# Half of layer 0's first feed-forward group as seven products, narrower score and value products, and an explicit order for the operand forms

## The chip, the cores and the metric

The kernel runs on one core of a Trainium2 chip. The engines of a core run side by side, each through its own instruction list: TensorE (PE, with its weight loads shown as PEld), VectorE (DVE), ScalarE (ACT), GpSimd (POOL) and SyncE (SP). SP and POOL also hold the queues from which transfers between HBM and on-chip memory (SBUF) are issued. TensorE adds its products up in PSUM, where the kernel keeps eight tiles of 512 floats per partition (banks). The metric is the device time of one execution in microseconds, the median of several runs.

## The reference

A trunk of two layers works on 512 tokens of width 1024. Each layer has eight stick-breaking attention heads and four differential attention heads, an output projection, and a feed-forward block of width 4096 with a squared ReLU. All data is float32.

```python
for l in range(DEPTH):
    h = rmsnorm(x, attn_norm[l])
    proj = jnp.einsum('bsd,de->bse', h, w_in[l])
    sb_q, sb_k, sb_v, df_q, df_k, df_v = jnp.split(proj, splits, axis=-1)
    sb_out = stick_breaking_attention(...)        # w = exp(log_beta + sums of log_keep), out = w v
    df_out = ...                                  # softmax(q1 k1) - lam * softmax(q2 k2), times v, rmsnorm
    x = x + jnp.einsum('bse,ed->bsd', mixed, w_o[l])
    h = rmsnorm(x, mlp_norm[l])
    u = jnp.square(jax.nn.relu(jnp.einsum('bsd,df->bsf', h, w_ff1[l])))
    x = x + jnp.einsum('bsf,fd->bsd', u, w_ff2[l])
return rmsnorm(x, final_norm)
```

## The kernel before

**Numbers.** Every operand of a product is held as two float32r tiles, `hi` (a rounded copy, made by ACT) and `lo` (what is left of the number, made by DVE). `three` (lines 294 to 299) issues hi·hi, hi·lo and lo·hi into one PSUM bank, so each product is three matmuls. A weight tile of 128x1024 floats comes by DMA and is split by `_Weights.split_part` (lines 117 to 132): ACT writes `whi` at line 115, DVE writes `wlo` at line 131. At most four split weights stand ahead of their use. ACT and DVE therefore do one split for every weight that PE uses.

**Layout.** x is kept transposed, as eight chunks of 128 features by 512 tokens. The attention part interleaves dense projections with attention steps by a written-out clock (`attn`, `dense`). A score product (`scores`, lines 522 to 529) for query block i is 128(i+1) keys wide, but at least 256. The transposed weights of keys 256 to 511 lie in `zh` and `zl`, whose first 128 columns are zeros (lines 346 to 348), so that the last value product (`s3`, line 634) is 256 wide as well.

**Feed-forward.** A layer's feed-forward is done in four groups of 1024 features. The second matrix of every group, and the first matrix of groups 1 to 3, are multiplied by a scheme that needs seven products of half-size blocks instead of eight. Each of the seven ("forms", named 11, x3, x2, 21, x1, x4, 22) has a weight that is one block or a sum or difference of blocks, and an activation that is one block or a combination too. `quad_group` (lines 1018 to 1065) does this for half a group's first matrix: seven forms in the order of `FORMS`, each of 8 x 3 matmuls that are 256 wide, into three banks X, V and Y. Between them ACT copies Y from X (line 1038), which has to be done before form x2 adds to X, and DVE and ACT form the squared ReLU and its combinations.

Group 0 does its first matrix plainly: eight blocks (`block`, lines 307 to 312) of 8 x 3 matmuls that are 512 wide. After each block `evict_whole` (lines 946 to 963) takes the ReLU, the square and the forms of the result, and `h_form` (lines 983 to 1006) makes a part of the activation forms that groups 1 to 3 need. In layer 0 these differences are written over x itself, which was saved to a DRAM tile `park` before (lines 939 to 941).

**Weights of the seven products.** `bring` (lines 876 to 890) fetches the five buffers a to e of one half group. Role "e" (the buffer `norms`, which held the sum of squares) is filled by a load from SP's queue and then by a second transfer that adds another block to it, issued from POOL's queue (line 888); role "b" (`first_b`) likewise. Form x3 uses e. Then DVE adds e to a (`add`, line 893), which gives x2's weight. The forms of the second matrix have adding transfers on the same POOL queue (`fetch`, line 856, for its x3; `grow`, line 863).

**Order.** A scheduler puts the instructions on the engines in an order that follows its own estimate of readiness; each engine then runs its list strictly in that order. `behind(a, b)` forces a to stand after b on its engine.

Of the kernel before, what the change touches and what calls it, by code (L numbers as in the profile page):

```python
# [36 lines left out]
MAN = ()  # L37
_CTX = {}
# [50 lines left out]
_FIRST = [(l, g, j, q) for l in range(L) for g in range(1, GROUPS) for j in range(2) for q in QUADS]  # L89


class _Weights:
    def __init__(self, nc, dram, rawp, splp):
        self.nc, self.dram, self.rawp = nc, dram, rawp
        self.loaded = self.split = self.used = self.turn = 0
        self.raw, self.tiles, self.home, self.then = {}, {}, {}, {}
        self.depth = 3
        self.limit = len(_RING) // L
        self.eager = False
        self.pools = [splp]  # L100
        self.owner = {}
        self.rest_of = {}
# [35 lines left out]
    def do_split(self, n, ahead=None):  # L138
        while self.split < min(n, len(_UNITS)):
            i = self.split  # L140
            kind = _UNITS[i][0]
            if ahead is not None and i > ahead and self.owner.get(self.spot(i), -1) >= ahead:
                break
            if kind not in "fs":
                self.load(_SLOT[i] + 1)
            self.split_part(i, 0, 1024)
            self.rest_of[i] = self.last[1]
# [16 lines left out]
def trunk(ctx, tc, opened, xT, w, w2, w1, gfin, lamv, cos, sin, out):  # L164
# [71 lines left out]
    def split(hi, lo, src):  # L236
        a = nc.scalar.activation(hi, src, AF.Copy)  # L237
        nc.vector.tensor_tensor(out=lo, in0=src, in1=hi.bitcast(F32), op=ALU.subtract)  # L238
        return a

    def split_less(hi, lo, src):
        a = nc.scalar.activation(hi, src, AF.Copy, scale=-1.0)
        nc.vector.scalar_tensor_tensor(
            out=lo, in0=src, scalar=-1.0, in1=hi.bitcast(F32), op0=ALU.mult, op1=ALU.subtract)
        return a
# [48 lines left out]
    def three(pt, a, b, first, last, goes_on=False):  # L294
        ah, al = a
        bh, bl = b
        nc.tensor.matmul(pt, ah, bh, start=first, stop=False, skip_group_check=goes_on)  # L297
        nc.tensor.matmul(pt, ah, bl, start=False, stop=False, skip_group_check=goes_on)  # L298
        nc.tensor.matmul(pt, al, bh, start=False, stop=last, skip_group_check=goes_on)  # L299
# [7 lines left out]
    def block(name, tag="mm"):  # L307
        pt = bank(tag, name)
        u = W.next("px" if name[0] == "p" else "1")
        for c in range(KC):  # L310
            three(pt, wpair(u, c), hpair(c), c == 0, c == KC - 1)
            yield pt if c == KC - 1 else None
# [20 lines left out]
    for l in range(L):  # L333
        with ExitStack() as actx:
# [11 lines left out]
            zh, zl = (ap_.tile([P, 512], F32R, tag=f"z{n}", name=f"z{n}{l}") for n in "hl")  # L346
            nc.gpsimd.memset(zh[:, 0:128].bitcast(F32), 0.0)
            nc.gpsimd.memset(zl[:, 0:128].bitcast(F32), 0.0)
# [256 lines left out]
            def s2(u, also):  # L605
# [11 lines left out]
                if half:  # L617
                    split(xh[:, 384:896], xl[:, 384:896], pts[0])
                    split(zh[:, 128:512], zl[:, 128:512], pts[1][:, 128:512])
# [122 lines left out]
            def wo(half):  # L742
                for j in range(4):
                    u = W.next("o")
                    for dd in range(2):
# [10 lines left out]
                        if half == 0:  # L756
                            make_h(db, gcol("mlp", l, db))
                            add_sq(db, db == 0, tt, nc.vector)
# [77 lines left out]
        with ExitStack() as fctx:  # L836
# [35 lines left out]
            groups = [(g, j) for g in range(1, GROUPS) for j in range(2)]  # L872
# [25 lines left out]
            def let_load():  # L898
                W.limit += len(_RING) // L if not last else 0
# [45 lines left out]

            def evict_whole(pt, k):
                pair, which = k // 2, k % 2
                F = spots["de"[pair % 2]].rearrange("p (a t) -> p a t", a=4)
                hi, lo = (e[:, :, pair % 2, :] for e in sides[pair // 2])
                t = F[:, 2 * which : 2 * which + 2, :].rearrange("p a t -> p (a t)")  # L950
                nc.scalar.activation(t, pt, AF.Relu)
                nc.scalar.activation(t, t, AF.Square)
                if which == 0:
                    split(hi[:, 0, :], lo[:, 0, :], F[:, 1, :])
                    return
                split(hi[:, 1:3, :], lo[:, 1:3, :], F[:, 2:4, :])
                tt2(F[:, 1, :], F[:, 1, :], F[:, 0, :], ALU.subtract)
# [19 lines left out]
            def scaled(out, c0, half, other, op):  # L977
                for c in range(4):
                    nc.vector.scalar_tensor_tensor(
                        out=out[:, c, :], in0=x[:, c0 + c, half], scalar=gcol("mlp", l, c0 + c), in1=other[:, c, :],  # L980
                        op0=ALU.mult, op1=op)

            def h_form(k):
                if k == 1:
                    for c in range(4):
                        nc.scalar.activation(ta[:, c, :], x[:, c, early], AF.Copy, scale=gcol("mlp", l, c))
                    if last:
                        scaled(tb_, 0, late_, ta, ALU.subtract)
                elif k == 2:
                    scaled(tc_, 4, early, ta, ALU.subtract)  # L990
                    if not last:
                        scaled(tb_, 0, late_, ta, ALU.subtract)
# [10 lines left out]
                for form, at in (("x3", 6 if last else 3), ("21", 7 if last else 5)):  # L1003
# [14 lines left out]
            def quad_group(g, j, banks_):  # L1018
# [8 lines left out]
                for form in FORMS:  # L1027
# [3 lines left out]
                    for pr in range(2):  # L1031
                        for c in range(4):
                            at = 512 * pr + P * c
                            three(to[:, 256 * pr : 256 * pr + 256], (u[0][:, at : at + P], u[1][:, at : at + P]),
                                  (h[0][:, c, :], h[1][:, c, :]),
                                  form in ("11", "x3") and pr == c == 0, pr == 1 and c == 3, True)
                    if form == "11":
# [26 lines left out]
                    if j and form in ("11", "x3", "x2"):  # L1064
# [113 lines left out]
            for g in range(GROUPS):  # L1178
# [7 lines left out]
                else:  # L1186
                    for k in range(2 * GP):
                        for n, pt in enumerate(block(f"f{l}_{g}_{k}", "any")):
                            if (k, n) == (1, 0):
                                rms_square(ssq, f"m{l}")  # L1190
                        evict_whole(pt, k)
                        h_form(k)
# [3 lines left out]
                    p_, q_, r_, s_ = ring[0] % 3, 3, (ring[0] + 1) % 3, (ring[0] + 2) % 3  # L1196
                    held_on = {"Y": [bank("t", f"Y{l}{r}") for r in range(2)], "V": [bank("mm", f"V{l}{r}") for r in range(2)]}
                chains = {"X": [temp(k, f"X{l}{g}{k}") for k in (p_, q_)], **held_on}
                for form in FORMS2:
# [47 lines left out]
                    if g and form in ("11", "x3"):  # L1247
# [113 lines left out]
```

## Time and profile before

| | |
|---|---|
| median of 3 runs | 1128.51 us (1127.95 to 1129.98) |
| profiled execution, whole time | 1129.41 us |
| profiled execution, span from first to last instruction | 1127.6 us |
| TensorE busy | 1118.6 us, 99% |
| VectorE busy | 904.9 us, 80% |
| ScalarE busy | 686.8 us, 61% |
| GpSimd busy | 148.1 us, 13% |
| DMA moved | 181.28 MB, 161 GB/s on average |

The busy time of an engine is the time in which at least one of its instructions runs. Matmuls overlap in the pipeline, so what one costs in a row of them is the distance from its start to the next one's, not its duration. "Idle before ... <-" in a row names what ended the engine's idle time before it.

### The profile page before, as it was taken

To read this page: it belongs to the slowest core of one execution; us is meant where nothing else is said; L and a number is where in the kernel's file an instruction comes from. 1 tells how busy PE (TensorE), PEld (TensorE's weight loads), DVE (VectorE), ACT (ScalarE), POOL (GpSimd) and SP (SyncE) were. 2 spreads that over 40 slices of the span, in tenths; PEclk is the share of its full clock that TensorE was granted. 3 is DMA by queue.
4 is the path that set the end of the run, shared out by engine and by line. 5 is a ranking of instruction groups with operands and counts; after the bars stand their busy time and mean duration, and the time that the engine had idled before them with its cause. 6 is when DMAs were issued, how large, how long until landed. Compare 5 with 4: busy or idle time off the path is not lost.

```text
span 1127.6 us, 17680 instructions
## 1 busy us (share of the span) xinstructions
PE 1118.6 (99%) x6613; PEld 990.2 (88%) x6613; DVE 904.9 (80%) x1317; ACT 686.8 (61%) x1115; POOL 148.1 (13%) x233
## 2 busy tenths in 40 slices
PE   9999999999999999999999999999999999999997
PEld 7899889878899899899888998898888998998986
DVE  7897788788658878779878977887876787797787
ACT  6456666567558458466344666665765484674665
POOL 1001343101011001001000013330010110010010
PEclk9999999999999999999999999999999999999999
DMA  7665363259777678757326643622477886687462
GB/s 253 157 181 150 88 175 103 76 192 242 191 205 178 174 209 179 190 139 206 112 75 187 169 132 112 166 78 75 149 183 218 209 187 178 184 187 202 116 131 94
DMA packets 61045, 181.28 MB, mean 161 GB/s; under 512 B 7456, under 2 KB 8736, under 8 KB 60960
## 3 DMA queue, kind: packets, MB, share of 16 engines
q1 hardware_dynamic: 50160, 141.84, 40.3%
q0 software_dynamic: 10368, 37.75, 19.2%
q8 instruction: 52, 0.85, 0.3%
q10 hardware_dynamic: 432, 0.56, 0.1%
q14 instruction: 33, 0.27, 0.1%
HBM read 150.77 MB, written 4.19 MB: 137 GB/s over the span
## 4 chain that ended last, share of the span: by engine, by line
PE 97%; DVE 1%; issue 1%; DMA 0%; ACT 0%; POOL 0%; SPq 0%; POOLq 0%; DVEq 0%
PE X L297 9%; PE X L298 9%; PE X L299 9%; PE V L297 4%; PE V L298 4%; PE V L299 4%; PE wo L297 3%; PE wo L299 3%; PE wo L298 3%; PE f L298 2%; PE f L299 2%; PE f L297 2%; PE Y L297 2%; PE Y L299 2%; PE Y L298 2%; PE W L299 1%
## 5 line engine op out<-in xcount | busy, mean ns | idle before, releaser
L115 ACT ACTIVATE whi<-q 128x1024 fp32r<-128x1024 f32 x96 | 101.6, 1059 | 109.8 <-PE X L299 37.9
L131 DVE TENSOR_TENSOR wlo<-q,whi 128x1024 fp32r<-128x1024 f32 x96 | 117.0, 1222 | 49.4 <-ACT whi L115 49.4
L115 ACT ACTIVATE whi<-raw 128x1024 fp32r<-128x1024 f32 (+1 forms) x82 | 80.9, 992 | 46.6 <-issue 20.3
L131 DVE TENSOR_TENSOR wlo<-raw,whi 128x1024 fp32r<-128x1024 f32 (+1 forms) x82 | 95.4, 1169 | 10.4 <-ACT whi L115 10.0
L297 PE MATMUL X<-whi,Ah 128*128 128x512 f32 x248 | 97.6, 394 | 0.0
L298 PE MATMUL X<-wlo,Ah 128*128 128x512 f32 x248 | 96.6, 390 | 0.0
L299 PE MATMUL X<-whi,Al 128*128 128x512 f32 x248 | 96.6, 389 | 0.0
L131 DVE TENSOR_TENSOR wlo<-waves,whi 128x1024 fp32r<-128x1024 f32 x40 | 48.9, 1222 | 17.0 <-ACT whi L115 16.8
L115 ACT ACTIVATE whi<-waves 128x1024 fp32r<-128x1024 f32 x40 | 42.2, 1055 | 31.0 <-PE X L299 18.2
L297 PEld LDWEIGHTS X<-whi,Ah 128*128 128x128 f32 x248 | 46.6, 188 | 11.9 <-DVE y L1091 1.9
L299 PEld LDWEIGHTS X<-whi,Al 128*128 128x128 f32 x248 | 46.6, 188 | 9.8
L298 PEld LDWEIGHTS X<-wlo,Ah 128*128 128x128 f32 x248 | 46.6, 188 | 8.8
L299 PE MATMUL X<-h_hi,wlo 128*128 128x256 f32 x192 | 54.3, 283 | 0.0
L297 PE MATMUL X<-hxh,whi 128*128 128x256 f32 x192 | 54.3, 283 | 0.0
L298 PE MATMUL X<-hxl,whi 128*128 128x256 f32 x192 | 54.3, 283 | 0.0
L299 PE MATMUL X<-hxh,wlo 128*128 128x256 f32 x192 | 54.3, 283 | 0.0
L298 PE MATMUL X<-h_lo,whi 128*128 128x256 f32 x192 | 54.3, 283 | 0.0
L297 PE MATMUL X<-h_hi,whi 128*128 128x256 f32 x192 | 54.3, 283 | 0.0
L298 PE MATMUL f<-h_lo,whi 128*128 128x512 f32 x128 | 49.9, 390 | 0.5 <-DVE h_lo L249 0.5
L297 PE MATMUL f<-h_hi,whi 128*128 128x512 f32 x128 | 50.4, 394 | 0.0
L299 PE MATMUL f<-h_hi,wlo 128*128 128x512 f32 x128 | 49.9, 390 | 0.0
L238 DVE TENSOR_TENSOR Al<-x,Ah 128x512 fp32r<-128x512 f32 (+1 forms) x60 | 46.6, 793 | 3.8 <-ACT Ah L237 3.5
(748 smaller groups left out, 3794.9 us busy)
## 6 DMA issues: line engine op xcount, KB each, us to landing
raw<-in_w SPq DMA_DIRECT2D x78, 512.0 KB, 3.8
q<-in_w SPq DMA_DIRECT2D x48, 512.0 KB, 4.8
q<-in_w POOLq DMA_DIRECT2D x48, 512.0 KB, 7.8
waves<-in_w SPq DMA_DIRECT2D x28, 512.0 KB, 4.9
first_a<-in_w SPq DMA_DIRECT2D x12, 512.0 KB, 4.4
first_b<-in_w SPq DMA_DIRECT2D x12, 512.0 KB, 5.2
first_c<-in_w SPq DMA_DIRECT2D x12, 512.0 KB, 4.3
first_b<-in_w POOLq DMA_DIRECT2D x12, 512.0 KB, 7.1
```

What stands on the lines that cost most here:

```text
L115: return self.nc.scalar.activation(o, src, AF.Copy)
L131: self.last = h, nc.vector.tensor_tensor(out=lo[:, a:b], in0=raw[:, a:b], in1=hi[:, a:b].bitcast(F32), op=ALU.subtract)
L238: nc.vector.tensor_tensor(out=lo, in0=src, in1=hi.bitcast(F32), op=ALU.subtract)
L297: nc.tensor.matmul(pt, ah, bh, start=first, stop=False, skip_group_check=goes_on)
L298: nc.tensor.matmul(pt, ah, bl, start=False, stop=False, skip_group_check=goes_on)
L299: nc.tensor.matmul(pt, al, bh, start=False, stop=last, skip_group_check=goes_on)
```

## The change

Half of group 0's first matrix in layer 0 becomes a `quad_group` too: `WHOLE = (4, 8)` says that layer 0 does four plain blocks instead of eight, and then one half group by seven products. Layer 1 keeps its eight blocks. The weights for the four blocks that go are no longer in the plain list; five buffers are brought by `bring(0, ...)` in their place, and because these would have carried the squared ReLU of the plain blocks, the `y` tiles take that instead (`spread`). In layer 0 the activation forms, spread over blocks 1 to 7 before, are made after blocks 0 to 3, and the forms of the squared ReLU later than before (`forms_of`, called with x3's block and inside `quad_group`). Score products of the first query block and the last value product become 128 wide, and the zero columns go; an unused tile `zpad` keeps their room. A number of `behind` calls fix the order of the new forms on ACT and DVE.

```diff
+WHOLE = (GP, 2 * GP)
...
+def _by_seven(l, g):
+    return range(0 if g else WHOLE[l] // GP, 2)
...
             if g == 0:
-                units.extend(("1", l, f) for f in range(2 * GP))
-            else:
-                units.extend(("s", l, g, j, form) for j in range(2) for form in FORMS)
+                units.extend(("1", l, f) for f in range(WHOLE[l]))
+            units.extend(("s", l, g, j, form) for j in _by_seven(l, g) for form in FORMS)
...
-            zh, zl = (ap_.tile([P, 512], F32R, tag=f"z{n}", name=f"z{n}{l}") for n in "hl")
-            nc.gpsimd.memset(zh[:, 0:128].bitcast(F32), 0.0)
-            nc.gpsimd.memset(zl[:, 0:128].bitcast(F32), 0.0)
+            zh, zl = (ap_.tile([P, 384], F32R, tag=f"z{n}", name=f"z{n}{l}") for n in "hl")
+            ap_.tile([P, 256], F32, tag="zpad", name=f"zpad{l}")
...
-                wd = P * (i + 1)
-                wp = max(wd, 256)
+                wp = P * (i + 1)
...
-                        (1, 2): ((zh, zl), 256, 256, 256), (1, 3): ((zh, zl), 0, 256, 256)}[(half, kb)]
+                        (1, 2): ((zh, zl), 128, 256, 256), (1, 3): ((zh, zl), 0, 384, 128)}[(half, kb)]
...
-            for k in (1, 2):
+            whole = WHOLE[l]
+            for k in (1, 2) if last else (1, 2, 3):
                 then(("1", l, k), skip)
-            for k, role in ((5, "a"), (6, "b"), (7, "c")):
-                then(("1", l, k), bring, 0, role)
-            then(("f", l, 0, "x2", 1), bring, 0, "e")
+            for k, role in enumerate("abc"):
+                then(("1", l, whole - 3 + k), bring, 0, role)
+            if last:
+                then(("f", l, 0, "x2", 1), bring, 0, "e")
+            else:
+                bring(0, "d")
...
             def h_form(k):
+                if last:
+                    form_late(k)
+                    return
+                if k == 0:
+                    for c in range(4):
+                        a = nc.scalar.activation(ta[:, c, :], x[:, c, early], AF.Copy, scale=gcol("mlp", l, c))
+                        behind(a, ends["h"][0])
+                    scaled(tc_, 4, early, ta, ALU.subtract)
+                    scaled(tb_, 0, late_, ta, ALU.subtract)
+                    split(*h_forms["x3"], tb_)
+                elif k == 1:
+                    scaled(td, 0, late_, tc_, ALU.add)
+                    split_less(*h_forms["x2"], td)
+                elif k == 2:
+                    scaled(te, 4, late_, td, ALU.subtract)
+                    split_less(*h_forms["22"], te)
+                else:
+                    split(*h_forms["x1"], tc_)
+                for form, c in ((("x3", 0),), (("x3", 1),), (("21", 0),), ())[k]:
+                    fetch(0, form, c)
...
-                    for k in range(2 * GP):
+                    for k in range(whole):
                         for n, pt in enumerate(block(f"f{l}_{g}_{k}", "any")):
                             if (k, n) == (1, 0):
                                 rms_square(ssq, f"m{l}")
+                                if not last:
+                                    bring(0, "e")
                         evict_whole(pt, k)
+                        if last:
+                            forms_of(k // 2, k % 2)
                         h_form(k)
+                        if not last and k > 1:
+                            forms_of(0, k == 3)
...
+                    if not last:
+                        p_, q_, r_, s_ = s_, r_, q_, p_
+                        quad_group(0, 1, (s_, r_, q_))
+                        rest_of_forms(1, "21")
```

More of the change, by code (lines that the diff above doesn't have):

```diff
@@ L88 @@
 _QUAD = [(l, g, q, c) for l in range(L) for g in range(GROUPS) for c in range(GP // 2) for q in QUADS]
-_FIRST = [(l, g, j, q) for l in range(L) for g in range(1, GROUPS) for j in range(2) for q in QUADS]
+_FIRST = [(l, g, j, q) for l in range(L) for g in range(GROUPS) for j in _by_seven(l, g) for q in QUADS]
+_SHARE = [sum(_UNITS[i][1] == l for i in _RING) for l in range(L)]
 class _Weights:
@@ L141, in do_split @@
             kind = _UNITS[i][0]
+            before = self.last if _UNITS[i - 1][:3] == ("s", 0, 0) else ()
             if ahead is not None and i > ahead and self.owner.get(self.spot(i), -1) >= ahead:
@@ L146, in do_split @@
             self.split_part(i, 0, 1024)
+            for a, b in zip(self.last, before):
+                self.behind(a, b)
             self.rest_of[i] = self.last[1]
@@ L296, in three @@
         bh, bl = b
-        nc.tensor.matmul(pt, ah, bh, start=first, stop=False, skip_group_check=goes_on)
-        nc.tensor.matmul(pt, ah, bl, start=False, stop=False, skip_group_check=goes_on)
-        nc.tensor.matmul(pt, al, bh, start=False, stop=last, skip_group_check=goes_on)
+        return (
+            nc.tensor.matmul(pt, ah, bh, start=first, stop=False, skip_group_check=goes_on),
+            nc.tensor.matmul(pt, ah, bl, start=False, stop=False, skip_group_check=goes_on),
+            nc.tensor.matmul(pt, al, bh, start=False, stop=last, skip_group_check=goes_on))
     def hpair(c):
@@ L310, in block @@
         for c in range(KC):
-            three(pt, wpair(u, c), hpair(c), c == 0, c == KC - 1)
+            W.product = three(pt, wpair(u, c), hpair(c), c == 0, c == KC - 1)[2]
             yield pt if c == KC - 1 else None
@@ L870, in then @@
                 W.then.setdefault(_INDEX[unit], []).append(lambda: fn(*args))
-            groups = [(g, j) for g in range(1, GROUPS) for j in range(2)]
+            groups = [(g, j) for g in range(GROUPS) for j in _by_seven(l, g)]
             spots = {"d": kept[(2, 1)], "e": norms.rearrange("p a t -> p (a t)")}
@@ L978, in scaled, with form_late @@
                 for c in range(4):
[L979 removed]
+                    a = nc.vector.scalar_tensor_tensor(
                         out=out[:, c, :], in0=x[:, c0 + c, half], scalar=gcol("mlp", l, c0 + c), in1=other[:, c, :],
                         op0=ALU.mult, op1=op)
+                    behind(a, ends["h"][1])
             def h_form(k):
+                if last:
[18 more added lines that the diff above has]
+                    fetch(0, form, c)
+            def form_late(k):
                 if k == 1:
                     for c in range(4):
[L986 to L988 removed]
+                        a = nc.scalar.activation(ta[:, c, :], x[:, c, early], AF.Copy, scale=gcol("mlp", l, c))
+                        behind(a, ends["h"][0])
+                    scaled(tb_, 0, late_, ta, ALU.subtract)
                 elif k == 2:
                     scaled(tc_, 4, early, ta, ALU.subtract)
[L991 to L992 removed]
                     split(*h_forms["x3"], tb_)
@@ L1002, in h_form @@
                     split(*h_forms["x1"], tc_)
-                for form, at in (("x3", 6 if last else 3), ("21", 7 if last else 5)):
+                for form, at in (("x3", 6), ("21", 7)):
                     if k == at:
@@ L1033, in quad_group @@
                             at = 512 * pr + P * c
-                            three(to[:, 256 * pr : 256 * pr + 256], (u[0][:, at : at + P], u[1][:, at : at + P]),
+                            one = three(to[:, 256 * pr : 256 * pr + 256], (u[0][:, at : at + P], u[1][:, at : at + P]),
                                   (h[0][:, c, :], h[1][:, c, :]),
                                   form in ("11", "x3") and pr == c == 0, pr == 1 and c == 3, True)
+                            if g == 0 and form == "11":
+                                behind(one[0], W.product)
                     if form == "11":
@@ L1063, in quad_group @@
                         nc.scalar.activation(F[3], F[3], AF.Square)
-                    if j and form in ("11", "x3", "x2"):
+                    if not g:
+                        if form in ("11", "x3"):
+                            forms_of(1, form == "x3")
+                    elif j and form in ("11", "x3", "x2"):
                         rest_of_forms(0, {"11": "21", "x3": "x2", "x2": "22"}[form])
@@ L1246, in trunk @@
                         came = gather(total, to)
-                    if g and form in ("11", "x3"):
+                    if (g or not last) and form in ("11", "x3"):
                         rest_of_forms(1, "x2" if form == "11" else "22")
```

40 lines of the change are left out of this document (25 added, 15 removed).

## The prediction

> **What bounds the kernel now.** I read the page first (busy times, slices, chain), then the order of time around layer 0's group 0, then the transfers.
>
> ```profile
> span 1127.6 us, 17680 instructions
> PE 1118.6 (99%) x6613; PEld 990.2 (88%) x6613; DVE 904.9 (80%) x1317; ACT 686.8 (61%) x1115; POOL 148.1 (13%) x233
> ...
> PEclk9999999999999999999999999999999999999999
> ...
> PE 97%; DVE 1%; issue 1%; DMA 0%; ACT 0%; POOL 0%; SPq 0%; POOLq 0%; DVEq 0%
> ```
>
> TensorE is the path: 99% busy, 97% of the chain, full clock. Whatever shortens its stream shortens the run, and any wait that it gets is added in full. What a matmul costs is the distance between starts, so I take 24 in a row of each width from the order of time (start, duration, engine, line).
>
> ```profile
> 285.57 0.39 PE L297 MATMUL X<-whi,Ah 128*128 128x512 f32 x1
> ...
> 291.01 0.39 PE L297 MATMUL V<-whi,Ah 128*128 128x512 f32 x1
> ...
> 439.94 0.28 PE L297 MATMUL X<-hxh,whi 128*128 128x256 f32 x1
> ...
> 442.81 0.40 PE L297 MATMUL X<-whi,Ah 128*128 128x512 f32 x1
> ```
>
> Width 512: 5.44 / 24 = 0.2267 us. Width 256: 2.87 / 24 = 0.1196 us. The next rows are the stage with the eight plain blocks (246 to 290) and one with seven-form work, then TensorE's one wait in the former.
>
> ```profile
> core 0: us, PE busy (x) PEld busy (x) DVE busy (x) ACT busy (x) POOL busy (x), PEclk, DMA share, GB/s
> 246.20:290.20 44.00, 43.78 (x195) 36.27 (x196) 37.68 (x66) 32.28 (x50) 6.33 (x7) 1.00 0.88 229
> 386.50:426.90 40.40, 40.40 (x275) 37.61 (x275) 29.59 (x31) 22.56 (x28) 4.39 (x5) 1.00 0.74 193
> ...
> 246.42 0.50 PE L298 MATMUL f<-h_lo,whi 128*128 128x512 f32 x1 [0.54 <-DVE h_lo L249]
> 247.70 0.60 PE L283 MATMUL rs_m<-edge,norms 128*128 128x128 f32 x4
> ```
>
> The stage that the change rebuilds is the tightest of the two: VectorE has 37.68 us of work in 44, the DMA engines are 88% busy. The 0.54 us wait before block 0 stays.
>
> **Blocks to forms.** Four blocks go, 4 x 24 products of width 512: 96 x 0.2267 = 21.76 us. Seven forms of 24 products of width 256 come: 168 x 0.1196 = 20.09 us. TensorE saves **1.67 us** if nothing is late.
>
> **Narrow products.** 64 score products and 56 value products (both layers) go from 256 to 128 columns. No product of these operands is that narrow in the trace. The same shape, 128x128, is found in transposes:
>
> ```profile
> L616 PE MATMUL T0s<-edge,sig0s 128*128 128x128 f32 x80 | 11.3, 272 | 0.0
> ...
> 205.07 0.77 PE T0s L616 x7
> ```
>
> 0.77 / 7 = 0.110 us each: halving the columns need not halve the time. Taken at that, 120 x (0.1196 - 0.110) = **1.2 us** saved. Ends: the line through the widths 512 and 256 gives 0.066 us at 128, 6.4 us saved; a loss isn't excluded, and the dearest row, width 512, bounds it at 120 x (0.2267 - 0.1196) = 12.9 us lost. I take the transposes, whose shape is the same. The Trainium skill ("TensorE: Matmul & The Clock Gate", Back-to-back issue gap) gives a sustained 81 ns for N=128 in a stream of weight loads and matmuls; by it the saving would be 4.6 us and the run 3.4 us shorter than my sum. The same sentence gives 131 ns for N=512, where this trace has 227, so I don't follow it.
>
> **The zeros' memsets** (four, 202 ns each) go, from an engine 13% busy: nothing.
>
> ```profile
> L347 POOL MEMSET zh<- 128x128 f32 x2 | 0.4, 202 | 9.1 <-PE yT L1108 9.1
> ```
>
> **The activation forms, moved earlier.** They were spread over blocks 1 to 7 and are now made after blocks 0 to 3: the same 16 scalings of 128x256 on VectorE and four on ScalarE, over x itself, so x must have been copied to `park`.
>
> ```profile
> park<-x SPq DMA_DIRECT2D x8, 256.0 KB, 2.1
> ...
> 241.54 3.37 SPq L941 DMA_DIRECT2D park<-x  x2
> ...
> 255.43 1.22 DVE L238 TENSOR_TENSOR hxl<-x,hxh 128x1024 fp32r<-128x1024 f32 x1
> ```
>
> The last copy is issued by 241.54 + 3.37 = 244.9 and lands 2.1 us later, at 247, as block 0 ends: no wait of note. x3's activation was complete at 255.43 + 1.22 = 256.7 although its scalings came one and two blocks later than now; TensorE asks for it at 266.7 (below). Cost nothing; the cover is 10 us. The forms of the squared ReLU move into the seven products (`forms_of`). They are asked for by the second matrix, 20 us behind the last block, so they cost nothing either, and the `behind` calls among them only place them; what they cost is in the queue that I count below. The two w2 adds stay on POOL's queue, one ahead of `norms`'s and one behind it; the latter is asked for by the second matrix as well. POOL's own sequencer waits at each add for its load, and nothing but adds is queued behind.
>
> **What the forms need.** Form x3 is the second of the seven and needs `norms`: a load, then an adding transfer on POOL's queue. Before, that pair was fetched in the middle of the second matrix and used after it. Now the load can only start once the sum of squares in `norms` has been transposed (247.70, early in block 1), and its add is the third on POOL's queue: `first_b`, then the w2 quad for x3, then `norms`. In transfers, four loads of plain weights go and five loads and two adds come, so five more transfers of 512 KB run in a stage that is 88% busy. The rows: the profile's transfers from 246 to 280 (count, size, median us to landing), the first two adds alone, the queues of the page (packets, MB, share of 16 engines) and the order of issue.
>
> ```profile
> q<-in_w SPq DMA_DIRECT2D x5, 512.0 KB, 6.3
> raw<-in_w SPq DMA_DIRECT2D x4, 512.0 KB, 5.4
> first_b<-in_w POOLq DMA_DIRECT2D x1, 512.0 KB, 5.8
> ...
> q<-in_w POOLq DMA_DIRECT2D x2, 512.0 KB, 9.0
> ...
> q1 hardware_dynamic: 50160, 141.84, 40.3%
> q0 software_dynamic: 10368, 37.75, 19.2%
> ...
> 247.12 0.81 SPq L854 DMA_DIRECT2D q<-in_w  x2
> 249.40 3.37 SPq L108 DMA_DIRECT2D raw<-in_w  x3
> ...
> 260.37 1.98 POOL L856 DMA_DIRECT2D q<-in_w  x2 [49.33 <-DVE waves L944]
> ```
>
> SP issues after the change, in the places of the rows at 247.12 and 249.40: two w2 quads, `first_b`, a quad, `norms`, a quad, then `first_c` and a quad. So `norms`'s load starts near 251 and lands at 251 + 6 = 257. One add with little beside it took 5.8 us: 263 is the early end for its landing. The late end is by engine time: q0's 19.2% of 1127.6 us over 72 adds is 3.0 us each, q1's 40.3% over 141.84 MB is 1.7 us per 512 KB; eight loads and three adds are 22.6 us from about 248.8, so 271.4. Without the last two loads it is 268. I take **268.5**, since two adds in a row already took 9.0 us each.
>
> **What waits for it.** Three things, in order. The last of four blocks ends at 285.57 - 4 x 5.44 = 263.8; form 11 fills TensorE to 266.7 (24 x 0.1196 = 2.87), x3 would end at 269.5. On ScalarE the split of `norms` stands ahead of ten instructions, the last of them the copy of Y that x2 must wait for. Their durations:
>
> ```profile
> L115 ACT ACTIVATE whi<-norms 128x1024 fp32r<-128x1024 f32 x12 | 12.7, 1061 | 10.0 <-PE W L299 10.0
> L237 ACT ACTIVATE Ah<-waves 128x512 fp32r<-128x512 f32 x8 | 4.7, 627 | 0.1
> L237 ACT ACTIVATE h_hi<-x 128x1024 fp32r<-128x1024 f32 x1 | 1.1, 1062 | 0.3 <-PE f L299 0.3
> L115 ACT ACTIVATE whi<-first_a 128x1024 fp32r<-128x1024 f32 x24 | 25.5, 1061 | 36.1 <-PE V L298 10.9 <-PE X L299 10.2 <-PE W L299 6.9
> L951 ACT ACTIVATE norms<-f 128x512 f32<-128x512 f32 x8 | 4.6, 578 | 0.0
> L952 ACT ACTIVATE norms<-norms 128x512 f32<-128x512 f32 x8 | 5.0, 628 | 0.1
> L115 ACT ACTIVATE whi<-waves 128x1024 fp32r<-128x1024 f32 x40 | 42.2, 1055 | 31.0 <-PE X L299 18.2 <-issue 5.3 <-DMA waves<-in_w 4.0
> L237 ACT ACTIVATE Ah<-waves 128x256 fp32r<-128x256 f32 x8 | 3.3, 410 | 0.1
> L1038 ACT COPY Y<-X 128x512 f32<-128x512 f32 x12 | 7.0, 581 | 0.0
> ```
>
> Split of `norms` 1.06, a form 0.63, x1's split 1.06, x2's weight 1.06, block 3's ReLU 0.58, a form 0.63, the square 0.63, 21's weight 1.06, two forms 0.82, the copy 0.58: 8.1 us. So x2 can start at 268.5 + 8.1 = 276.6 instead of 269.5: TensorE loses **7.1 us**, in pieces: some 3 us before x3's first products, 1.2 us before those with `wlo`, the rest before x2. With the landing at 263 it is 1.6 us, at 271.4 10 us. VectorE gets three more splits of a weight and two additions of buffers in this stage:
>
> ```profile
> L131 DVE TENSOR_TENSOR wlo<-q,whi 128x1024 fp32r<-128x1024 f32 x96 | 117.0, 1222 | 49.4 <-ACT whi L115 49.4
> ```
>
> 5 x 1.22 = 6.1 us, 43.8 us of work in a stage of about as many: it has no slack left, but the next stages (29.59 in 40.40) take up a delay, so I add nothing. Were that cover gone, up to these 6.1 us would show.
>
> **Sum.** -1.67 - 1.2 + 7.1 = +4.2 us on the profiled execution's 1129.41: 1133.6. The median of the runs, 1128.51, is 0.9 below that execution, which gives 1132.7, **1133 us**. Its own range is 1129 to 1137.
>
> **Rivals.**
> (a) The add is in time. If `norms` has landed by 269.5 - 8.1 = 261.4, nothing waits and the sum is -2.9: **1125.6**. For it: POOL is free, 13% busy. Against: with the load landing at 257 the add would have to take 4.4 us, less than the 5.8 of the row, third in a queue. With a landing before 262 the change is faster.
> (b) Narrow products are dear. At the cost of width 512 they lose 12.9 us instead of gaining 1.2: 1133 + 14.1 = **1147**. For it: the kernel pads exactly these to 256, with a column of zeros, and its trace has no narrower one. Against: the transposes.
> (c) Narrow products are cheap, on the line through the wider ones at 0.066 us: 1133 - 5.2 = **1128**. For it: 512 and 256 differ by 0.107, an even price per column if nothing else binds. Against: 0.110 in the transposes. (By the skill's 81 ns it would be 1129.6.)
> (d) The clock falls. TensorE would idle for about 3 us twice within 8 us, where its wait in this stage was 0.54 us; if its products then go at half pace for as long as it idled, that costs half of each 3 us, in all 1.5 to 3 us: **1135**. Against: the clock row, which shows no dip. The skill's page on the clock gate (Part 1) says that an idle window of about 3.4 us halves the clock until a busy one has passed; no run here shows it yet.
>
> **How the numbers follow.** My forecast 0.45, (a) 0.13, (b) 0.17, (c) 0.12, (d) 0.13. A measurement here tells 0.2%, 2.3 us, from no change. Faster (under 1126.2): (a). Same (to 1130.8): (c) and 0.06 of mine. Slower: the rest. The range 1128 to 1148 leaves out (a) and the upper end of (b).
>
> **What would show it.** Right: x3's first product in V starts late behind ScalarE's split of `norms`, that split waits for a DMA, and x2's first product in X waits for ScalarE's copy Y. Blocks: 96 fewer products of width 512. Narrow products: the distance between starts at width 128, near 0.110. Wrong: no idle TensorE in layer 0's group 0, or 128-wide products at 0.23 or at 0.07.

## The result and the profile after

The changed kernel took 1138.91 us (median of four, 1136.53 to 1139.48) beside 1128.67 us for the kernel before: a ratio of 1.0083, 95% interval 1.0071 to 1.0095. Measured again beside other kernels it took 1136.88 against 1129.27 (1.0068, 1.0054 to 1.0081). So it lost 8 to 10 us where 4 were forecast. Its profiled execution took 1139.17 us, 9.76 us more than that of before.

Three lines of its page (span, PE's busy time, the clock in 40 slices):

```profile
span 1137.3 us, 17823 instructions
PE 1121.9 (99%) x6685; PEld 995.3 (88%) x6685; DVE 913.2 (80%) x1316; ACT 690.0 (61%) x1115; POOL 150.2 (13%) x231
PEclk9999999998999999999999999999999999999999
```

Busy time grew by 3.3 us, the span by 9.7. And the clock row has an 8 in the tenth slice, where before had nines throughout. TensorE's waits of layer 0's group 0 between 250 and 300 us:

```profile
engine line waited for: us in total, times, longest us
PE V L304 <- ACT whi L120: 3.8, 1, 3.8
PE X L304 <- ACT Y L1084: 1.8, 1, 1.8
PE V L306 <- DVE wlo L136: 0.9, 1, 0.9
```

These are the three waits at the places that the prediction named (in order of time: V at L304, V at L306, X at L304). ScalarE's order of time shows their cause, the split of `norms` 9.5 us after the instruction before it, and the copy of Y ten instructions later:

```profile
260.24 0.63 ACT L964 ACTIVATE y<-y 128x512 f32<-128x512 f32 x1
270.40 1.06 ACT L120 ACTIVATE whi<-norms 128x1024 fp32r<-128x1024 f32 x1 [9.53 <-DMA norms<-in_w]
...
275.62 0.63 ACT L245 ACTIVATE Ah<-y 128x512 fp32r<-128x512 f32 x1 [1.26 <-DVE y L953]
...
278.35 0.58 ACT L1084 COPY Y<-X 128x512 f32<-128x512 f32 x1
```

TensorE's own order of time:

```profile
264.65 0.28 PE L304 MATMUL X<-h_hi,whi 128*128 128x256 f32 x1
...
267.40 0.28 PE L306 MATMUL X<-h_hi,wlo 128*128 128x256 f32 x1
271.51 0.39 PE L304 MATMUL V<-hxh,whi 128*128 128x256 f32 x1 [3.83 <-ACT whi L120]
...
272.89 0.58 PE L306 MATMUL V<-hxh,wlo 128*128 128x256 f32 x1 [0.87 <-DVE wlo L136]
...
278.98 0.39 PE L304 MATMUL X<-hxh,whi 128*128 128x256 f32 x1 [1.75 <-ACT Y L1084]
...
280.17 0.42 PE L305 MATMUL X<-hxl,whi 128*128 128x256 f32 x1
280.38 0.41 PE L306 MATMUL X<-hxh,wlo 128*128 128x256 f32 x1
```

Form 11 starts at 264.65, x3 at 271.51, x2 at 278.98, 14.33 us after form 11 where two forms take 5.75. The last two rows are products of width 256 that stand 0.21 us apart, not 0.12: half pace. That is rival (d), and it came on top of the forecast, not in its place.

Where the 9.76 us lie, by starts of the same products in both profiled executions (first of `p0w`, first transpose of the second norm `rs_m`, first of `yT`, first of `half`, all from the order of time):

| stretch | before | changed | difference |
|---|---|---|---|
| start to `p0w` | 16.97 | 17.23 | +0.26 |
| `p0w` to `rs_m` (attention, layer 0) | 230.73 | 231.29 | +0.56 |
| `rs_m` to `yT` (group 0 and the groups behind it) | 307.83 | 316.48 | +8.65 |
| `yT` to `half` (layer 1) | 559.87 | 560.15 | +0.28 |

### The profile page after: what moved, and what is told of

Read it like the earlier page. It is cut to its first block, busy times and chain, and to the rows that moved or that the text cites. A ratio compares the mean times of both kernels' runs of the same rounds, so it can differ in the third digit from the quotient of the medians.

```text
span 1137.3 us, 17823 instructions
## 1 busy us (share of the span) xinstructions
PE 1121.9 (99%) x6685; PEld 995.3 (88%) x6685; DVE 913.2 (80%) x1316; ACT 690.0 (61%) x1115; POOL 150.2 (13%) x231
## 3 DMA queue, kind: packets, MB, share of 16 engines
q1 hardware_dynamic: 50304, 142.37, 40.0%
q0 software_dynamic: 10656, 38.80, 19.1%
## 4 chain that ended last, share of the span: by engine, by line
PE 71%; DMA 3%; DVE 2%; ACT 1%; issue 1%; POOL 0%; POOLq 0%; DVEq 0%; SPq 0%; ACTq 0%
PE X L304 9%; PE X L305 9%; PE X L306 9%; PE V L304 4%; PE V L305 4%; PE V L306 4%; PE Y L305 2%; PE Y L304 2%; PE Y L306 2%; PE f L306 1%; PE f L305 1%; PE f L304 1%; PE wo L304 1%; PE wo L305 1%; PE wo L306 1%; DMA norms<-in_w 1%
## 5 line engine op out<-in xcount | busy, mean ns | idle before, releaser
L120 ACT ACTIVATE whi<-raw 128x1024 fp32r<-128x1024 f32 (+1 forms) x78 | 76.8, 990 | 47.4 <-issue 16.9
L304 PE MATMUL X<-whi,Ah 128*128 128x512 f32 x248 | 97.8, 394 | 0.0
L306 PE MATMUL X<-whi,Al 128*128 128x512 f32 x248 | 96.7, 390 | 0.0
L304 PE MATMUL X<-hxh,whi 128*128 128x256 f32 x208 | 59.7, 287 | 1.8 <-ACT Y L1084 1.8
L305 PE MATMUL X<-hxl,whi 128*128 128x256 f32 x208 | 59.7, 287 | 0.0
L306 PE MATMUL X<-hxh,wlo 128*128 128x256 f32 x208 | 59.6, 287 | 0.0
L305 PE MATMUL X<-h_lo,whi 128*128 128x256 f32 x208 | 58.9, 283 | 0.0
L306 PE MATMUL X<-h_hi,wlo 128*128 128x256 f32 x208 | 58.9, 283 | 0.0
L304 PE MATMUL X<-h_hi,whi 128*128 128x256 f32 x208 | 58.9, 283 | 0.0
L304 PEld LDWEIGHTS X<-whi,Ah 128*128 128x128 f32 x248 | 46.6, 188 | 12.0 <-DVE y L1140 1.9
L306 PEld LDWEIGHTS X<-whi,Al 128*128 128x128 f32 x248 | 46.6, 188 | 9.9
L120 ACT ACTIVATE whi<-first_a 128x1024 fp32r<-128x1024 f32 x26 | 27.5, 1059 | 36.1 <-PE V L305 10.9
L136 DVE TENSOR_TENSOR wlo<-first_a,whi 128x1024 fp32r<-128x1024 f32 x26 | 31.8, 1225 | 21.5 <-ACT whi L120 21.5
L245 ACT ACTIVATE Ah<-x 128x512 fp32r<-128x512 f32 (+1 forms) x65 | 46.1, 709 | 2.1 <-DVE x L953 1.7
```

Of the source, the lines that this page charges most:

```text
L120: return self.nc.scalar.activation(o, src, AF.Copy)
L136: self.last = h, nc.vector.tensor_tensor(out=lo[:, a:b], in0=raw[:, a:b], in1=hi[:, a:b].bitcast(F32), op=ALU.subtract)
```

## The experiments

Theory A: the late landing of `norms`, then ScalarE's queue, hold x2 back; the idle time lets the clock fall; narrow products are worth nothing in sum. The rivals stand in the expectations. All ratios are against the kernel before on the same chip.

### Each part alone

```diff
 # e1_narrow: into before
-                wd = P * (i + 1)
-                wp = max(wd, 256)
+                wp = P * (i + 1)
...
-  (1, 2): ((zh, zl), 256, 256, 256), (1, 3): ((zh, zl), 0, 256, 256)}
+  (1, 2): ((zh, zl), 128, 256, 256), (1, 3): ((zh, zl), 0, 384, 128)}
 # e2_seven: the same lines taken back out of the changed kernel
```

> The kernel before, with the narrow score and value products alone. In the trace of the changed kernel the narrow products start 0.10 us apart on average (0.061 where another narrow one follows, 0.11 before a wide one), which alone would save 120 x (0.1196 - 0.10) = 2.3 us; but TensorE reached the output projection 0.5 us later against the start of the projections in layer 0, and 0.2 us later in layer 1. Theory A (the narrow products let TensorE run ahead of the transfers and splits that it then waits for, so the saving is given back inside the attention): 1128.7 + 0.7 = 1129.4, within 0.1% of before. Theory B (the offset in the attention is scatter between executions and the saving is real): 1126.4. The term of the prediction (0.110 us each): 1127.5.

> The changed kernel without the narrow products: score and value products are 256 wide again, with their zero columns. Theory A: all that the change costs is in the first group, -1.7 us from the products, +7.2 us of waits and +2.9 us of products at half clock: 1128.7 + 8.4 = 1137.1, 0.7% slower than before. Rival (the narrow products save their 2.3 us): the changed kernel plus that, 1141. The prediction's sum without the clock: 1134.

Measured: narrow alone 1129.48 us, 1.0001 (0.9992 to 1.0010). Seven products alone 1134.85 us, 1.0055 (1.0041 to 1.0069): 2.2 us less than Theory A had said, mostly because the half pace cost nothing that counts in it (below). The narrow products were forecast to save 1.2 us; alone they save nothing that can be told from 0, within 1 us. Two orders of time show why. First a pair of score products between wide ones, narrow alone:

```profile
112.25 0.23 PE L526 MATMUL S0s<-st0s0k,st0s0q 128*128 128x128 f32 x1
112.31 0.27 PE L527 MATMUL S0s<-kl0s0k,st0s0q 128*128 128x128 f32 x1
112.42 0.33 PE L436 MATMUL p0u<-whi,h_hi 128*128 128x256 f32 x1
112.58 0.28 PE L437 MATMUL p0u<-wlo,h_hi 128*128 128x256 f32 x1
```

and the same pair 256 wide, in the run with the seven products alone:

```profile
112.33 0.28 PE L535 MATMUL S0s<-st0s0k,st0s0q 128*128 128x256 f32 x1
112.45 0.29 PE L536 MATMUL S0s<-kl0s0k,st0s0q 128*128 128x256 f32 x1
112.58 0.28 PE L444 MATMUL p0u<-whi,h_hi 128*128 128x256 f32 x1
112.69 0.28 PE L445 MATMUL p0u<-wlo,h_hi 128*128 128x256 f32 x1
```

The narrow pair starts 0.06 and 0.11 us apart, but the wide product after it takes 0.16 instead of 0.12. Pair and next product take 0.33 us against 0.36: 0.015 us saved a narrow product, near the forecast's 0.110 us each. Summed over layer 0's attention in these two executions, distances between starts: score products 0.90 us less and value products 0.83 less, but projections 0.86 more, the transposes of the weights 0.55 more, the output projection 0.40 more. So 1.73 us are saved by 60 products, and 1.26 are lost in the wide products behind them, those of the projections and of the output projection, each some 0.05 us longer; what is left is 0.47 us, or 0.008 a product, close to the forecast's 0.01. The transposes take it back. Their part is in the main a wait for VectorE, as here, where seven of them take 1.03 us from 212.11 to 213.14 (0.69 in before, from 204.90 to 205.59): the weight loads of the last three start when VectorE's split `xl`, which reads an earlier `T0s`, is done. First the narrow products alone, then before:

```profile
212.11 1.28 PE L614 MATMUL T0s<-edge,sig0s 128*128 128x128 f32 x7
212.83 0.31 PEld L614 LDWEIGHTS T0s<-edge,sig0s 128*128 128x128 f32 x3 [0.37 <-DVE xl L238]
213.14 0.47 PE L297 MATMUL wo<-mdh,whi 128*128 128x512 f32 x1
```

```profile
204.90 0.93 PE L616 MATMUL T0s<-edge,sig0s 128*128 128x128 f32 x7
205.59 0.47 PE L297 MATMUL wo<-mdh,whi 128*128 128x512 f32 x1
```

The scheduler goes by its estimate of the products' time, so narrower ones also gave ScalarE and VectorE another order: 75 of ScalarE's and 114 of VectorE's instructions stand elsewhere than in before. What the prediction had not seen either: the 0.54 us wait before block 0 that should have stayed is gone in the changed kernel and in each part alone. No run settles why.

### The early weight

```diff
 # e3_early: into the changed kernel
+                if role == "e" and not last:
+                    spots["e"] = (norms if n else y[(0, 0)]).rearrange("p a t -> p (a t)")
...
+                bring(0, "e")
                 bring(0, "d")
...
-                                if not last:
-                                    bring(0, "e")
 # e7_early_seven: the same, into e2_seven
```

> The changed kernel with one thing moved: the first weight of form x3 is loaded and added up in a tile of the output (y 00, not written before the second matrix), which is free some 25 us before norms is. Theory A (the late landing of norms is the root of both waits and of the fall of the clock): no wait of note before x3 or x2, full clock throughout, 1128.7 - 1.7 + 0.7 = 1127.7. Rival (ScalarE's and VectorE's queues hold x2 back by themselves, since they have 8 us of work between that split and the copy of Y): a wait of 2 to 4 us before x2 stays, 1130 to 1132.

> The kernel before with seven products in half of layer 0's first group, the first weight of x3 in the output tile 00 and no narrow products: the candidate that could beat both. Theory A (narrow products are worth nothing, the seven products 1.7 us once nothing waits): 1127.3, 0.15% faster than before, the same as the run with narrow products and the early weight. Rival (narrow products in company of the seven cost 1.4 us in the attention, as the profiled executions of the three kernels with both read): 1126.6 to 1127.0, and visibly below the run with both.

Measured: 1128.04 us, 0.9990 (0.9982 to 0.9999), and without narrow products 1126.59 us, 0.9975 (0.9965 to 0.9985): the fastest, with the narrow scores alone (below), and faster than both kernels. The first is near Theory A's 1127.7, with no wait in group 0. The second is at its rival's end: narrow products beside the seven seem to cost something, which is taken apart below. The stretch in question in windows, the kernel with the early weight and narrow products (us; TensorE busy and count, then the other engines, the granted clock, the DMA share, GB/s):

```profile
246.20:262.70 16.50, 16.50 (x76) 13.64 (x75) 16.50 (x29) 12.72 (x18) 2.63 (x3) 1.00 0.96 307
262.70:300.00 37.30, 37.30 (x245) 34.34 (x244) 35.55 (x48) 28.71 (x41) 5.24 (x6) 1.00 0.85 188
```

TensorE never stands still, at full clock, with VectorE busy for 35.55 of 37.30 us. The load is issued at 220.25 instead of 250.56 us, and its add lands at 232.15. One buffer's time of becoming free was the root of all three waits. ScalarE's ten instructions alone hold nobody back when they can be spread over the stage. `rs_m` to `yT` takes 306.31 us (306.35 without narrow products): the seven products save 1.5 us once nothing waits. The rest of e7's 2.7 us is mostly the attention up to `rs_m`, 229.75 us instead of 230.73, without the wait before block 0. That part isn't the seven products' merit: narrow products alone have 229.96 there.

### The clock

```diff
 # e4_fill: into the changed kernel
                 for form in FORMS:
+                    if not g and form in ("x3", "x2"):
+                        for _ in range({"x3": 16, "x2": 8}[form]):
+                            behind(nc.tensor.matmul(fill, zeros[:, 0:128], zeros[:, 128:640], start=True, stop=True), one[2])
                     u = W.next("s")
```

A few more `behind` calls keep the order of the other engines, but for two pairs of ScalarE's instructions.

> The changed kernel with 24 products of zeros that nobody reads, 16 where TensorE waits for form x3 and 8 where it waits for x2, some 0.22 us each; the waits for data stay as they are. Theory A (the clock falls because TensorE stood idle): with idle time filled, no product at half pace, and 2.9 us less than the changed kernel: 1136.0. Rival (the wide spacing of the products behind the waits has another cause, as transfers or weight loads that come late): unchanged, 1138.9, or more by what the fillers delay.

Measured: 1137.11 us, 1.0068 (1.0055 to 1.0081), beside 1.0083 and 1.0068 for the changed kernel. No product at half pace, as Theory A says. But the gain depends on where the half pace lies. In windows of 3.41 us laid on the edges of the half-pace stretches, the changed kernel's first profile:

```profile
265.93:269.35 3.42, 1.75 (x15) 1.55 (x13) 0.00 (x0) 0.00 (x0) 0.00 (x0) 1.00 1.07 212
269.35:272.76 3.41, 0.50 (x2) 0.30 (x2) 2.29 (x2) 2.36 (x3) 0.00 (x0) 1.00 0.62 121
272.76:276.17 3.41, 3.28 (x15) 3.28 (x16) 3.25 (x6) 2.15 (x5) 0.00 (x0) 0.50 0.53 154
276.17:279.58 3.41, 1.66 (x14) 1.45 (x13) 3.41 (x7) 3.41 (x8) 0.87 (x1) 1.00 0.32 37
279.58:282.99 3.41, 3.41 (x19) 3.41 (x18) 3.41 (x6) 2.59 (x4) 0.00 (x0) 0.50 0.89 173
```

and the same kernel again, e8_again:

```profile
264.08:267.49 3.41, 2.57 (x22) 2.36 (x20) 0.00 (x0) 0.00 (x0) 0.00 (x0) 1.00 1.07 219
267.49:270.90 3.41, 0.31 (x2) 0.30 (x2) 1.35 (x2) 1.42 (x2) 0.00 (x0) 1.00 0.91 180
270.90:274.31 3.41, 2.60 (x13) 2.35 (x12) 3.25 (x5) 2.53 (x4) 0.00 (x0) 0.50 0.39 97
274.31:277.72 3.41, 2.72 (x13) 2.42 (x12) 3.41 (x6) 3.02 (x6) 0.87 (x1) 0.50 0.16 62
277.72:281.13 3.41, 3.08 (x25) 3.08 (x26) 3.41 (x6) 3.41 (x6) 0.00 (x0) 1.00 0.95 157
```

Half pace before x2's start only shortens the wait for the copy of Y, and costs nothing: with fillers, and no half pace, x2 starts 8.60 us after the landing of `norms`, as in both executions of the changed kernel. Behind x2's start it costs in full: 1.57 us in the first execution (17 products of some 0.212 instead of 0.1196 us). In the second it was over at 277.72, before x2 started at 278.06; the 0.1 us lost there is x2's first product alone, which takes 0.22 us behind a wait, with fillers and full clock too (e4).

### The queues

```diff
 # e5_first: into the changed kernel
-                for form, c in ((("x3", 0),), (("x3", 1),), (("21", 0),), ())[k]:
+                for form, c in ((), (("21", 0),), (("x3", 0),), (("x3", 1),))[k]:
...
                                     bring(0, "e")
+                                    late.pop()()    # first_b's adding transfer
 # e6_defer: into the changed kernel
-                        if not last and k > 1:
-                            forms_of(0, k == 3)
...
-                        if form in ("11", "x3"):
-                            forms_of(1, form == "x3")
+                        if form in ("x3", "x2", "21", "x1"):
+                            forms_of(*{"x3": (0, 0), "x2": (0, 1), "21": (1, 0), "x1": (1, 1)}[form])
```

> The changed kernel with the adding transfer of norms as the first on POOL's queue: the one of first_b and the two of the second matrix's x3 are issued behind it, and the loads of the latter as well. Theory A (norms lands late because it stands third in that queue, 12.3 us after its issue where the first in the queue took 9): norms lands 2.5 to 6 us earlier against the start of form 11, the start of x2 with it, and the products run at full clock: 1130 to 1134. Rival (the DMA engines are full whatever the order, so the landing hardly moves): 1138.9.

> The changed kernel with the forms of the squared ReLU of the plain blocks made two to three forms later, so that five of the instructions between the split of norms and the copy of Y, 2.7 us of them (0.61, 0.61, 0.40, 0.42 and, of the square, 0.62), stand behind that copy or are spread. Theory A (once norms has landed, ScalarE's queue sets the start of x2): x2 starts 2 us earlier against the landing, 1136.9. Rival (VectorE's wlo of x2's weight sets it, or the square that the copy waits behind): less than 0.7 us gained, 1138.2 to 1138.9.

> The changed kernel itself beside the others, for their comparison on one chip. Theory A: 1138.9 again, norms landing 5.5 to 6 us after the start of form 11, and a fall of the clock near 270 or 280 us; TensorE reaches the transposes of the second norm at 246.5 to 248.5, and if the 1.4 us of late transfers in the attention belong to the kernel they are there again, if they are scatter they are gone.

Measured: e5 1135.16 us (1.0053, 1.0040 to 1.0066), e6 1134.26 us (1.0047, 1.0034 to 1.0059), the changed kernel beside them 1136.88. In e5 the scheduler kept `first_b`'s add in front; `norms` moved up from third to second, ahead of both adds of the second matrix. Its waits, then those of e6:

```profile
266.27 0.39 PE L304 MATMUL V<-hxh,whi 128*128 128x256 f32 x1 [0.44 <-ACT whi L120]
267.53 0.39 PE L306 MATMUL V<-hxh,wlo 128*128 128x256 f32 x1 [0.76 <-DVE wlo L136]
274.53 0.58 PE L304 MATMUL X<-hxh,whi 128*128 128x256 f32 x1 [4.12 <-ACT Y L1089]
```

```profile
269.61 0.39 PE L304 MATMUL V<-hxh,whi 128*128 128x256 f32 x1 [3.38 <-ACT whi L120]
270.99 0.55 PE L306 MATMUL V<-hxh,wlo 128*128 128x256 f32 x1 [0.87 <-DVE wlo L136]
```

Each takes one of the two big waits away, though in e5 the other grows from 1.75 to 4.12 us. How the terms add up, in profiled executions (us; landing and start of x2 counted from the start of form 11; slow products: what products behind x2's start take beyond 0.1196 us each, of which the first one behind a wait takes 0.10 at full clock, and the rest is half pace; the sum is 306.33 + (x2 - 5.75) + that column, with 306.33 from e3 and e7):

| kernel | `norms` lands | x2 starts | slow products | sum | `rs_m` to `yT` |
|---|---|---|---|---|---|
| changed | 5.73 | 14.33 | 1.57 | 316.48 | 316.48 |
| again (e8) | 5.84 | 14.44 | 0.11 | 315.13 | 315.13 |
| seven alone (e2) | 5.36 | 13.96 | 0.10 | 314.64 | 314.64 |
| filled (e4) | 5.98 | 14.58 | 0.10 | 315.26 | 315.29 |
| queue (e5) | 2.34 | 11.74 | 2.42 | 314.74 | 314.69 |
| forms later (e6) | 5.28 | 12.02 | 0 | 312.60 | 312.59 |
| early (e3) | before its use | 5.75 | 0 | 306.33 | 306.31 |

The landing (e5: 3.5 us earlier, x2 2.7 earlier than in e8) and ScalarE's queue (e6: 1.9 us less between landing and x2) are both real terms. But e5's edit moved loads too, and against e8 the place in the queue is the smaller part: its add is issued 8.18 us before form 11, in e8 5.06, mostly because the load of `norms` landed 5.85 us after its issue instead of 8.49. From issue to landing the add takes 10.52 us in e5 and 10.90 in e8, 12.29 in the changed kernel's first profile. Theory A's expectation for e5 fails at "full clock": with the one wait of 4.12 us right before x2 come 6.8 us at half pace (272.99 to 279.82), 2.42 us lost behind x2's start, and most of the gain in the stage with them. In e8 the landing and the fall of the clock (at 270.89) came as expected, the time was 2.0 us below the 1138.9.

### Narrow scores and narrow values apart

```diff
 # e9_scores: into e7_early_seven
-                wp = max(wd, 256)
+                wp = P * (i + 1)
 # e10_values: into e7_early_seven
-  (1, 2): ((zh, zl), 256, 256, 256), (1, 3): ((zh, zl), 0, 256, 256)}
+  (1, 2): ((zh, zl), 128, 256, 256), (1, 3): ((zh, zl), 0, 384, 128)}
```

> The seven products with the early weight (1126.6), and the score products alone 128 wide for the first query block. Theory A (a narrow pair costs 0.111 us a product, its 0.05 us on the next product included, so 64 scores save 64 x (0.1196 - 0.111) = 0.55 us if no engine's order shifts): 1126.0. Rival (the narrow scores are what costs the 1.4 us between the run with the early weight and narrow products and the one without them): 1127.3 to 1128.0.

> The same with the value products alone 128 wide. Theory A (56 products of 0.104 us with what they add to the next one would save 0.9 us, but the new order on ScalarE and VectorE brings the two waits of transposes, 0.25 and 0.29 us a layer, that all runs with narrow products have): 1126.3 to 1127.0. Rival (the value products cost the 1.4 us): 1127.5 to 1128.0.

> Both, once more, beside them on the same chip. Theory A: the 1.4 us over 1126.6 are late transfers between tiles at the first scores (0.5 to 1.2 us in four of seven profiled executions with narrow products, in none without) and the waits of transposes: 1127.5 to 1128.0 again, with a wait for st0d or kl0d in the profile in about half the executions. Rival (scatter between the two jobs): 1126.0 to 1126.6, below the two single ones.

Measured: scores 1127.28 us, 0.9975 (0.9965 to 0.9984); values 1128.36 us, 0.9990 (0.9981 to 0.9999); both (e3 again) 1127.44 us, 0.9984 (0.9975 to 0.9993). Against e7's 0.9975, narrow scores give nothing, and narrow values seem to cost some 1.7 us (0.0015 of 1129), but the intervals overlap. In the profiled executions the values alone cost e10 0.86 us in layer 0's attention and 0.57 in layer 1: in the former they save 0.90 us of value products, the transposes take 0.86 us more, the projections 0.52 and the output projection 0.31. That points to the rival for the values, by the mechanism that Theory A named, but isn't clear of scatter; and with the scores narrow too (e11) that attention takes 229.93 us, against 230.61 in e10 and 229.75 in e7. So it seems to hang on the order that the engines get, not on the products alone. What stays open as well: four of eight profiled executions with both kinds of narrow products lose 0.8 to 1.6 us more in layer 0's attention, where the first score products wait for a transfer between tiles that lands late (the changed kernel, e3, e4, e8), and none of the three with wide ones does. Whether the products' new times expose a delay that is always there was not settled.

## Why the prediction was right, and where its sizes were off

- **TensorE is the path, waits count in full**: right; the sum in the table gives each stage to 0.05 us from starts of products alone.
- **Blocks to forms, -1.67 us**: 1.5 measured.
- **Narrow products, -1.2 us**: the price, 0.110 us each, was right as an average, but by luck: transposes in a row stand 0.109 us apart, whereas narrow products stand 0.06 and 0.11 apart and cost the next one 0.05. Rivals (b) and (c) are refuted: the 0.06 within a pair is paid for by the next product. The term failed at what the prediction didn't say: whether another engine then comes late. Transposes wait for VectorE's splits, and the sum is +0.1 us (1.0001) alone. The Trainium skill's 81 ns ("TensorE: Matmul & The Clock Gate", Back-to-back issue gap) doesn't hold for these products either: 0.06, 0.11, and 0.05 more behind them.
- **What the forms need**: the mechanism was right. Its "five more transfers" are three by its own count (five loads and two adds for four loads), and the page's bytes grew by three (q1 from 141.84 to 142.37 MB, q0 from 37.75 to 38.80); no term hangs on it. The landing was 270.4, 5.73 us after form 11's start, where 268.5 - 263.8 = 4.7 was forecast: 1.0 us short. Rival (a) would have needed 261.4.
- **What waits for it, 7.1 us**: the three waits and their releasers were right. From landing to x2 it took 278.98 - 270.38 = 8.6 us, 8.1 forecast, because ScalarE itself waits for VectorE in between. With the landing, x2 starts 8.6 us late, 1.5 more than forecast.
- **The clock**: in the first profile the largest miss within the stage. As a rival it had 1.5 to 3 us; the trace has 1.57 us that count (0.10 of them the first product behind the wait) and some 1.3 that hide in a wait. It should have been a term of the sum, from 0.1 to 2.4 us by where the windows fall.
- **Costs put at nothing** (memsets, activation forms, VectorE's 6.1 us): right; e3 holds all of them without a wait in group 0.
- **The 0.54 us before block 0 stays**: wrong, it went.

In sum, for the two profiled executions of the changed kernel: -1.5 for the blocks, +8.6 and +8.7 for the waits, 1.6 and 0.1 for slow products, and +1.1 and -0.2 for the rest of the kernel (start, attention and layer 1) give 9.8 and 7.1 us. The medians gave 10.2 and 7.6. So the direction and its cause were right, while the loss was about twice the 4.2 us of the forecast: of the two medians, 1138.91 lies outside the forecast's own range of 1129 to 1137, and 1136.88 just inside. Only the wider range, stretched for rival (b), held both.

## What to carry to other kernels

Before you put a cheaper scheme earlier in a stage, ask when the buffers become free that its operands live in: here a tile that was free 30 us earlier turned a loss of 5.8 us (seven products alone) into a gain of 2.7. A wait of 2 to 4 us on the bound engine can cost more than its length through the clock (1.75 us in the changed kernel, 4.12 in e5), and the extra counts where no later wait absorbs it. A shorter instruction on the bound engine is worth only what the engines that work beside it can follow; take its price from a whole group with the product after it, not from the distance of two starts.

## What the runs showed of the hardware

The granted clock moves in windows of 3.41 us, and the two fences under "The clock" show a rule that the stages with waits of all six such profiles follow. At full clock, a window with TensorE busy for 1.66 of 3.41 us or less (0.49) was followed by half pace, and one with 1.75 (0.51) or more wasn't. At half pace, busy for 2.60 of 3.41 (0.76) wasn't enough to come back, and 3.28 (0.96) was; 2.72 (0.80) was followed by full clock too. So an idle stretch of 1.76 us, half a window, can do it (277.22 to 278.98 in the changed kernel), and whether it does depends on where the window's edges fall. That made 1.46 us of difference between the two profiled executions of the changed kernel; how much of the whole spread, 1134.75 to 1139.48 us, it explains isn't shown. Nor is the edge near a half sharp. At the end of the seven products alone, a window with 0.46 busy was followed by full clock:

```profile
1124.80:1128.21 3.41, 1.58 (x14) 1.37 (x12) 2.10 (x7) 2.62 (x9) 1.08 (x2) 1.00 0.70 267
1128.21:1131.63 3.42, 0.00 (x0) 0.00 (x0) 0.78 (x2) 0.62 (x1) 0.00 (x0) 1.00 0.82 307
```

The Trainium skill ("TensorE: Matmul & The Clock Gate", Part 1) has the same window of 3413 ns, free-running, which these runs bear out; it asks for an idle window, where 0.49 busy was enough here.
